# Weight units in another order, small products with a break between their halves, and a bias added by a product, in a mixer-and-experts layer

## The chip, the cores and the metric

The kernel runs on one core of a Trainium2 chip. The metric is the time of one execution on the device in microseconds (us); three runs of the kernel before are given below. The engines go by the names of the profile: PE is TensorE's matmul stream (PEld its loads of weights), DVE is VectorE, ACT is ScalarE, POOL is GpSimd, SP is SyncE, which issues most DMA transfers.

## The reference

The layer works on 256 latent and 256 context tokens of 1024 features, all in fp32. A vector `c` gives six modulation rows (`ada_mod`). Two bidirectional recurrent branches of four heads each (mLSTM and HGRN2) mix the tokens, a gate merges them, and a mixture of 32 experts follows, four per token.

```python
def ada_mod(cvec, w, b):
    return jnp.split(jax.nn.silu(cvec) @ w + b, 6, axis=-1)

# mixer_features: one projection, split into the branches' inputs
    p = h @ w_in + b_in
    mqk, mv, mo, hq, hi, hg, hf, ga, gb, mg = jnp.split(p, SPLIT_POINTS, axis=-1)
    ...
    hi = split_heads(hi, N_HEADS_H).astype(f32)
    z = hf.astype(f32).reshape(B, T, 2, W_H)
    ...
        logf = jnp.logaddexp(jnp.log(lb_d), jnp.log1p(-lb_d) + jax.nn.log_sigmoid(zd))
        kk = (1 - lb_d) * jax.nn.sigmoid(-zd)

# hgrn_scan, per chunk of 32 tokens
        A = jnp.cumsum(fc, axis=2)
        S_new = jnp.exp(AL)[..., None] * S + jnp.einsum('bhsd,bhsv->bhdv', kc * jnp.exp(AL[:, :, None] - A), ic)
        diff = jnp.where(mask[:, :, None], A[:, :, :, None, :] - A[:, :, None, :, :], -jnp.inf)
        s = jnp.einsum('bhtsd,bhsd->bhts', qc[:, :, :, None, :] * jnp.exp(diff), kc)
        o = jnp.einsum('bhts,bhsv->bhtv', s, ic) + jnp.einsum('bhtd,bhdv->bhtv', qc * jnp.exp(A), S)

# layer
        x = x + g1[:, None, :] * rmsnorm(yl, norm_mix_post[l])
        hl = modulate(rmsnorm(x, norm_ffn_pre[l]), sh2, sc2)
        x = x + g2[:, None, :] * rmsnorm(moe_ffn(hl, ...), norm_ffn_post[l])
```

## The kernel before

The mixer takes the first 410 us or so, routing follows, and then the experts' weights stream through until the end. The change lies in the mixer.

**Weight units.** The projection `h @ w_in` is cut into units of 1024 x 256 weights, listed by `unit(...)` and run in that order by the loop of line 1104. A unit's weights are loaded by SyncE, split into a high part (a cast on ScalarE, line 226) and a low part (a difference on VectorE or GpSimd, line 228), and multiplied in two blocks of products (line 237, `mm`). An `hf` block is 24 products of 512 columns; its PSUM bank is emptied by ScalarE (`ev_hf`; for the units of this change line 506, which adds a bias). An `hi` or `mv` block is 48 products of 256 columns, and an `hi` block's bank is emptied by VectorE (`ev_hi`, line 511, a sum into `hi_sb`). A block can begin when one of the rotating banks is empty: two banks named `mm` and, outside the units 7 to 10, the one named `am`.

**Steps of other work.** Behind each block the loop calls `step(n)`, which takes n pieces from the generators in the list `work`, each up to its next `yield`. `hgrn_head(h)` is such a generator. It makes the running sums A (lines 534 and 535) and G on VectorE, differences X (lines 560 and 561), their exponentials on ScalarE (line 562) and products with q and k (lines 582 and 583); the weights' decay Y on ScalarE (lines 567 to 569); then products on TensorE: transposes `trh`, the context's state `so`, the off-diagonal blocks `pts`, and for each of two chunks 44 products of 32 x 32 into `db`, of which VectorE's mask and sum make the diagonal of `pt`; last the output `ho`, emptied into `hmh` (line 639). `to_hgrn` prepares the heads 0 and 1 (on ScalarE: gates and logarithms), `first_heads` puts them into `work`, and `last_heads`, called by `to_last`, does the same for heads 2 and 3 (line 516 is their logarithm).

**Late modulation.** In the units 7 to 10 the generator `ada_rest` makes the last four modulation rows: 16 loads of `w_ada` (line 191) and 16 groups of four products each (line 196) into the bank `am`, eight groups for each half. At the end of a half VectorE adds the bias rows, which lie in `ada_sb`, to the bank (line 855). The first group of the second half needs the bank to be read.

**Engine queues.** Each engine works in the order in which its instructions were written, so a waiting instruction holds back all behind it.

Of the kernel before, what the change touches and what calls it, by code (L numbers as in the profile page):

```python
# [19 lines left out]
KB = 8  # L20
# [44 lines left out]
def layer_kernel(ctx: ExitStack, tc, x, ctxt, w_ada, b_ada, n_mix_post, n_ffn_post, w_in, b_in, w_pa, w_pb, w_out,  # L65
                 w_router, b_router, w_gu, b_gu, w_dn, b_dn, consts, vecs, out, dbg=None):
    nc = tc.nc
# [19 lines left out]
    ident = cp.tile([P, P], F32, name="ident")  # L87
# [103 lines left out]
        nc.sync.dma_start(w, w_ada[k * P:(k + 1) * P, c0:c0 + 2048])  # L191
        return w

    def ada_mm(bank, w, k):
        for j in range(4):
            nc.tensor.matmul(bank[32 * j:32 * j + 32, :], cs[:, k, :], w[:, 512 * j:512 * j + 512],
                             start=(k == 0), stop=(k == KB - 1), skip_group_check=True)

    banks = []

# [243 lines left out]
    work = []  # L444
# [85 lines left out]
    def hgrn_head(h):  # L530
# [82 lines left out]
        pt = hq_.tile([P, 4, P], F32, name="pt", tag="pt", bufs=1)  # L613
        nc.scalar.activation(pt, pts, AF.Identity)
        for ch in range(2):
            db = psm.tile([P, NTERM, 32], F32, name="db", tag="A", bufs=2)
            for tm in range(NTERM):
                for j in range(4):
                    a = ch * P + 32 * j
                    if tm < NTERM - 1:  # L620
                        l_ = r_ = X[:, tm % 2, 2 + tm // 2, a:a + 32]
                    else:
                        l_, r_ = ks[:, a:a + 32], q[:, a:a + 32]
                    nc.tensor.matmul(db[32 * j:32 * j + 32, tm], l_, r_, start=True, stop=True)
            dm = hq_.tile([P, NTERM, 32], F32, name="dm", tag="dm", bufs=1)
            nc.vector.tensor_mul(dm, db, lmask)
            ds_ = hq_.tile([P, 32], F32, name="ds_", tag="ds_", bufs=2)
            nc.vector.tensor_reduce(ds_, dm.rearrange("p n t -> p t n"), AX.X, OP.add)
            for j in range(4):
                sl = slice(32 * j, 32 * j + 32)  # L630
                nc.vector.tensor_copy(pt[sl, 3 * ch, sl], ds_[sl])
# [213 lines left out]
    def ada_rest():  # L845
        for i in range(8):
            nc.gpsimd.dma_start(ada_sb[32 * (i % 4):32 * (i % 4) + 1, i // 4, :],
                                b_ada[2048 + 512 * i:2560 + 512 * i].rearrange("(a b) -> a b", a=1))
        for hf in range(2):
            b = pmm.tile([P, 512], F32, name="am", tag="am", bufs=1)  # L850
            for k in range(KB):
                ada_mm(b, ada_load(2048 + 2048 * hf, k), k)
                if k < KB - 1:
                    yield
            nc.vector.tensor_add(ada_sb[:, hf], ada_sb[:, hf], b)
            yield

    def block_of(a, k):
# [66 lines left out]

    for u in (mq_[1], hf_[0], mk_[0], hf_[1], mk_[1]):
        unit(*u)
    unit(*hi_[0], to_hgrn)
    unit(*hi_[1], None, first_heads)
    unit(*hf_[2])  # L930
    unit(*hf_[3])
    unit(*mv_[0], to_last)
    unit(*mv_[1])

# [169 lines left out]
    for i, u in enumerate(units[1:], 1):  # L1104
# [4 lines left out]
        for j, blk in enumerate(u[1](*cur)):  # L1109
            blk()  # L1110
            for _ in range(rest_at.get((i, j), 0)):
                next(rest)
            if len(convs) > 2 or i > 0 and convs:
                with after(mods[-1:]):
                    convs.pop(0)()
            step(2 if work and len(work) <= 2 or i > 11 else 1)
            for f, *args in load_at.get((i, j), ()):
                if not gu_first:
                    step(100)
                    M["stack"].close()  # L1120
                    vps.close()
                    fps.close()
                    wr1 = pool("wr1", stack=moe)
                    rl = pool("rl", stack=moe)
                    hb0, hb2 = (rl.tile([P, 2, D], BF, name=n) for n in ("hb0", "hb2"))
                f(*args)
# [779 lines left out]
```

## Time and profile before

| | |
|---|---|
| three runs | 1362.54, 1362.87, 1364.57 us; median 1362.87 us |
| profiled execution | 1364.41 us, of which its span is 1362.6 us |
| TensorE busy | 1265.5 us, 93% of the span; mean granted clock 0.981 |
| VectorE, ScalarE, GpSimd busy | 41%, 27%, 10% |
| DMA | 474.12 MB, mean 348 GB/s |

The span goes from the first to the last instruction; 1.8 us of the execution lie outside it. A busy share is an average over stages with different limits, so the stages have to be looked at one by one; the granted clock is the share of full speed that TensorE was given.

### The profile page before, as it was taken

How to read it: one execution, taken by the hardware profiler on the slowest of the kernel's cores; microseconds unless marked ns; L12 is line 12 of the kernel's file. 1: busy time of each engine (PE TensorE's matmuls, PEld its weight loads, DVE VectorE, ACT ScalarE, POOL GpSimd, SP SyncE). 2: the span in 40 equal slices, each digit the busy share in tenths (PEclk: the TensorE clock that was granted, in tenths of full speed). 3: DMA queues.
4: the chain of work that ended last, by engine and by line, in shares of the span. 5: the costliest groups of instructions: out<-in, count | busy, mean ns of one | idle time of the engine just before them, and what ended most of it. 6: DMA issues, size and time to landing. Idle time of an engine off the chain costs nothing. (4 is left out here: it accounts for less than half of the span.)

```text
span 1362.6 us, 20982 instructions
## 1 busy us (share of the span) xinstructions
PE 1265.5 (93%) x8719; PEld 637.9 (47%) x8719; DVE 561.8 (41%) x1211; ACT 361.8 (27%) x712; POOL 129.6 (10%) x140
## 2 busy tenths in 40 slices
PE   4998877999998899999999999999999999999995
PEld 2788665799993333333333333333333333333321
DVE  4699477787666332322222222222222222222224
ACT  3557362446643321111111111211121111211102
POOL 4543335300110000000000000000000000000000
PEclk9999988999999899999999999999999999999997
DMA  9731625745889989999999999999999999999994
GB/s 324 242 102 63 202 78 195 260 135 195 309 304 395 390 367 422 430 424 427 427 427 427 425 392 429 426 426 426 429 424 427 426 428 427 425 428 426 427 420 163
DMA packets 78424, 474.12 MB, mean 348 GB/s; under 512 B 6048, under 2 KB 45480, under 8 KB 50672
## 3 DMA queue, kind: packets, MB, share of 16 engines
q1 hardware_dynamic: 77936, 472.54, 85.7%
q8 instruction: 70, 1.15, 0.3%
q14 instruction: 34, 0.28, 0.1%
q0 software_dynamic: 384, 0.15, 0.0%
HBM read 471.60 MB, written 1.07 MB: 347 GB/s over the span
## 5 line engine op out<-in xcount | busy, mean ns | idle before, releaser
L1609 PE MATMUL pg<-wc,hmh 128*64 128x512 f32 x1048 | 271.8, 598 | 14.9 <-DMA wc<-in_w_gu_dram 14.4
L1609 PE MATMUL pu<-wc,hmh 128*64 128x512 f32 x1048 | 268.9, 592 | 0.0
L1659 PE MATMUL dnl<-wc,hmh 128*64 128x512 f32 x1056 | 236.0, 598 | 9.4 <-ACT hmh L1640 9.1
L1659 PEld LDWEIGHTS dnl<-wc,hmh 128*64 128x64 f32 x1056 | 73.6, 137 | 169.1 <-issue 135.4
L1651 DVE TENSOR_TENSOR ys<-dnl,ys 128x512 fp32r<-128x512 f32 x32 | 22.1, 692 | 307.2 <-ACT ys L1650 307.2
L1609 PEld LDWEIGHTS pu<-wc,hmh 128*64 128x64 f32 x1048 | 74.4, 137 | 150.5 <-issue 150.5
L1620 ACT ACTIVATE scr<-scr 128x512 f32<-128x512 f32 (+1 forms) x34 | 21.0, 619 | 465.8 <-DVE scr L1619 465.8
L1609 PEld LDWEIGHTS pg<-wc,hmh 128*64 128x64 f32 x1048 | 66.9, 136 | 145.5 <-issue 107.4
L1675 DVE SCALAR_TENSOR_TENSOR xr<-sc,wv,xr 128x512 f32<-128x512 f32 x124 | 87.4, 747 | 109.5 <-PE sc L1669 109.5
L1619 DVE TENSOR_SCALAR scr<-pg 128x512 f32<-128x512 f32 (+1 forms) x34 | 22.9, 676 | 219.7 <-PE pg L1609 219.7
L237 PE MATMUL mm<-xh,wp 128*128 128x256 f32 (+1 forms) x576 | 107.7, 332 | 4.2 <-DVE hi_sb L511 3.1
L237 PEld LDWEIGHTS mm<-xh,wp 128*128 128x128 f32 x576 | 88.0, 196 | 14.8 <-issue 4.1
L1385 ACT ACTIVATE hmh<-xp,s2c,a2c 128x64 f32<-128x64 f32 x264 | 81.5, 414 | 38.6 <-PE xp L1581 33.2
L1717 POOL TENSOR_TENSOR scr<-xr,g2n 128x512 f32<-128x512 f32 x2 | 2.5, 1266 | 908.2 <-issue 908.2
L1650 ACT CAST ys<-dnl 128x512 fp32r<-128x512 f32 x32 | 18.7, 585 | 232.3 <-PE dnl L1659 232.3
L1581 PEld LDWEIGHTS <-hb 128*128 128x128 bf16 x960 | 43.7, 98 | 24.3 <-issue 24.3
L228 DVE TENSOR_TENSOR wp<-w,wp 128x2048 fp32r<-128x2048 f32 x21 | 48.0, 2288 | 13.4 <-ACT wp L226 13.4
L237 PE MATMUL mm<-xl,wp 128*128 128x256 f32 (+1 forms) x288 | 53.2, 328 | 0.0
L1669 PE MATMUL sc<-ys,ohT 64*128 64x512 f32 x256 | 48.3, 450 | 4.0 <-DVE xr L1673 3.1
L226 ACT CAST wp<-w 128x2048 fp32r<-128x2048 f32 x25 | 47.5, 1900 | 15.6 <-PE mm L237 8.1
L1581 PE MATMUL xp<-oh,hb 128*128 128x64 bf16 x960 | 47.2, 193 | 0.0
L237 PEld LDWEIGHTS mm<-xl,wp 128*128 128x128 f32 x288 | 44.4, 196 | 4.2
(625 smaller groups left out, 1529.4 us busy)
## 6 DMA issues: line engine op xcount, KB each, us to landing
wc<-in_w_gu_dram SPq DMA_DIRECT2D x119, 2048.0 KB, 25.2
wc<-in_w_dn_dram SPq DMA_DIRECT2D x63, 2048.0 KB, 25.2
w<-in_w_in_dram SPq DMA_DIRECT2D x26, 1024.0 KB, 5.3
w<-in_w_ada_dram SPq DMA_DIRECT2D x16, 1024.0 KB, 4.9
wc<-in_w_gu_dram SPq DMA_DIRECT2D x16, 1024.0 KB, 27.0
aw<-in_w_ada_dram SPq DMA_DIRECT2D x8, 1024.0 KB, 11.7
w<-in_w_pa_dram SPq DMA_DIRECT2D x2, 1024.0 KB, 5.3
w<-in_w_out_dram SPq DMA_DIRECT2D x2, 1024.0 KB, 6.6
```

Source lines behind the costliest of these rows:

```text
L226: nc.scalar.copy(hi, w)
L228: eng.tensor_tensor(lo, w, hi.bitcast(F32), op=OP.subtract)
L237: nc.tensor.matmul(o, ls[k][a], rs[k][b], start=(i + k == 0), stop=(i == 2 and k == n - 1))
L1385: nc.scalar.activation(xg[:, k], xp[k], AF.Identity, scale=a2c[:, k:k + 1], bias=s2c[:, k:k + 1])
L1581: nc.tensor.matmul(xp[:, k], part[:, ch, k * P:(k + 1) * P], oh[:, ch], start=(i == 0), stop=(i == 5))
L1609: nc.tensor.matmul(banks[u][n * g:n * g + n, :], xg[:, k], rows_[:, c0:c0 + W], start=False, stop=(k == KB - 1), skip_group_check=True)
L1619: nc.vector.tensor_scalar(g_, cut(banks[0], i), 7.0, None, op0=OP.min)
L1620: nc.scalar.activation(s_, g_, AF.Sigmoid, scale=1.702)
L1651: nc.vector.tensor_sub(ys[1], b, ys[0].bitcast(F32))
L1659: nc.tensor.matmul(b[64 * hf:64 * hf + 64, :], aT_[:, j, g], dn[g][:, j, hf * 512:hf * 512 + 512], start=(g == 0 and j == 0), stop=(g == 1 ...
L1669: nc.tensor.matmul(s[hf], ohT[ps_, ch * P:(ch + 1) * P], ys[i][ps_], start=(i == 0), stop=(i == 1))
L1675: nc.vector.scalar_tensor_tensor(dst, s[hf], wv[:, ch, col:col + 1], dst, op0=OP.mult, op1=OP.add)
```

## The change

Four edits. The units `hf_[2]` and `hf_[3]` stand ahead of `hi_[0]` and `hi_[1]`, not behind them; `to_hgrn` is called ahead of the first of the moved pair as before of the first of the other, and `first_heads` ahead of `hi_[0]`, where before it was called behind `hi_[1]`. A `yield` stands ahead of each of a head's two runs of 44 small products, so that a head has two pieces more, and in the units 8 to 11 the loop takes three pieces behind a block. In `ada_rest` the bias rows are brought into the bank by a product with the identity ahead of the first group, and ScalarE copies the finished bank, where VectorE added the bias.

```diff
-    def ada_mm(bank, w, k):
+    def ada_mm(bank, w, k, first=True):
         for j in range(4):
             nc.tensor.matmul(bank[32 * j:32 * j + 32, :], cs[:, k, :], w[:, 512 * j:512 * j + 512],
-                             start=(k == 0), stop=(k == KB - 1), skip_group_check=True)
+                             start=(first and k == 0), stop=(k == KB - 1), skip_group_check=True)
...
         for ch in range(2):
+            yield
             db = psm.tile([P, NTERM, 32], F32, name="db", tag="A", bufs=2)
...
             b = pmm.tile([P, 512], F32, name="am", tag="am", bufs=1)
+
+            nc.tensor.matmul(b, ident, ada_sb[:, hf], start=True, stop=False, skip_group_check=True)
             for k in range(KB):
-                ada_mm(b, ada_load(2048 + 2048 * hf, k), k)
+                ada_mm(b, ada_load(2048 + 2048 * hf, k), k, False)
                 if k < KB - 1:
                     yield
-            nc.vector.tensor_add(ada_sb[:, hf], ada_sb[:, hf], b)
+            nc.scalar.copy(ada_sb[:, hf], b)
             yield
...
-    unit(*hi_[0], to_hgrn)
-    unit(*hi_[1], None, first_heads)
-    unit(*hf_[2])
+    unit(*hf_[2], to_hgrn)
     unit(*hf_[3])
+    unit(*hi_[0], first_heads)
+    unit(*hi_[1])
     unit(*mv_[0], to_last)
     unit(*mv_[1])
...
-            step(2 if work and len(work) <= 2 or i > 11 else 1)
+            step(3 if 8 <= i <= 11 else 2 if work and len(work) <= 2 or i > 11 else 1)
```

Line numbers of the changed kernel are one higher from the new `yield` on, and three higher behind `ada_rest`.

**ScalarE, behind head 0's exponentials of X.** Of before: `csg` is a gate of the mLSTM's keys, the cast makes high parts of weights, Y is head 0's decay.

```order
L747 ACT_TABLE_LOAD
L747 ACTIVATE csg<-kT 128x512
L293 ACT_TABLE_LOAD
L226 CAST wp<-w 128x2048
L567 ACTIVATE Y<-A 128x256
L568 ACTIVATE Y<-A 128x128
L569 ACTIVATE Y<-A 128x128
L567 ACTIVATE Y<-A 128x256
L568 ACTIVATE Y<-A 128x128
L569 ACTIVATE Y<-A 128x128
L226 CAST wp<-w 128x2048
L506 ACTIVATE lf_660<-mm,cols 128x512
```

And of the change, at the same place:

```order
L748 ACT_TABLE_LOAD
L748 ACTIVATE csg<-kT 128x512
L293 ACT_TABLE_LOAD
L506 ACTIVATE lf_660<-mm,cols 128x512
L226 CAST wp<-w 128x2048
L567 ACTIVATE Y<-A 128x256
L568 ACTIVATE Y<-A 128x128
L569 ACTIVATE Y<-A 128x128
L567 ACTIVATE Y<-A 128x256
L568 ACTIVATE Y<-A 128x128
L569 ACTIVATE Y<-A 128x128
L506 ACTIVATE lf_660<-mm,cols 128x512
```

The emptyings of `hf` banks (line 506) have moved ahead: the second of them stands ahead of the cast, the third directly behind Y. The first product of the unit `hi_[0]` waits for the third.

**TensorE, small products of heads 0, 1 and 2.** Before, at head 0, with the first product of its output behind:

```order
L624 MATMUL db<-xr 32x32 x40
L624 MATMUL db<-hqT,ks 32x32 x4
L624 MATMUL db<-xr 32x32 x40
L624 MATMUL db<-hqT,ks 32x32 x4
L635 MATMUL ho__1604<-hi_sb,pt 128x128
```

And of the change, at head 0:

```order
L625 MATMUL db<-xr 32x32 x40
L625 MATMUL db<-hqT,ks 32x32 x4
L625 MATMUL db<-xr 32x32 x40
L625 MATMUL db<-hqT,ks 32x32 x4
L237 MATMUL mm<-wp,xh 128x256 x8
```

A block of an `hi` unit follows where the output followed; the 88 products of head 0 stand together as before. Of the change, at the beginning of head 1's:

```order
L625 MATMUL db<-xr 32x32 x14
L596 MATMUL so<-hi_sb,kt 128x128 x4
L600 MATMUL pts<-Y 128x128
L625 MATMUL db<-xr 32x32 x19
L601 MATMUL pts<-Y 128x128
L605 MATMUL pts<-xr 64x64
```

And of the change, at head 2's, with groups of the late modulation (`am`) and blocks of an `mv` unit:

```order
L625 MATMUL db<-xr 32x32 x17
L196 MATMUL am<-w,cs 32x512 x4
L625 MATMUL db<-xr 32x32 x23
L625 MATMUL db<-hqT,ks 32x32 x4
L237 MATMUL mm<-wp,xh 128x256 x8
L237 MATMUL mm<-wp,xl 128x256 x4
L196 MATMUL am<-w,cs 32x512 x4
L237 MATMUL mm<-wp,xl 128x256 x4
L237 MATMUL mm<-wp,xh 128x256 x16
L237 MATMUL mm<-wp,xl 128x256 x8
L237 MATMUL mm<-wp,xh 128x256 x8
L625 MATMUL db<-xr 32x32 x33
```

The products of head 1 and head 2 stand in pieces now. In the kernel before, those of head 1 stand together, as those of head 0 do.

**VectorE, at head 2's differences X.** Of before, around the first read of an `mv` block's bank into `v_sb`:

```order
L560 TENSOR_TENSOR xr<-A 128x2x64
L561 TENSOR_TENSOR xr<-A 128x2x64
L560 TENSOR_TENSOR xr<-A 128x4x32
L561 TENSOR_TENSOR xr<-A 128x4x32
L560 TENSOR_TENSOR xr<-A 128x8x16
L757 TENSOR_TENSOR v_sb<-mm,bvi 128x2x128 x2
L561 TENSOR_TENSOR xr<-A 128x8x16
L560 TENSOR_TENSOR xr<-A 128x16x8
```

And of the change, from head 2's first running sum on:

```order
L534 SCALAR_TENSOR_TENSOR A<-scm_667,lf_660 128x256
L541 SCALAR_TENSOR_TENSOR G<-cons_669,lf_660 128x255
L560 TENSOR_TENSOR xr<-A 128x2x64
L535 SCALAR_TENSOR_TENSOR A<-scm_668,lf_660 128x256
L542 SCALAR_TENSOR_TENSOR G<-cons_669,lf_660 128x255
L561 TENSOR_TENSOR xr<-A 128x2x64
L560 TENSOR_TENSOR xr<-A 128x4x32
L758 TENSOR_TENSOR v_sb<-mm,bvi 128x2x128 x2
L561 TENSOR_TENSOR xr<-A 128x4x32
```

The read into `v_sb` stood behind 19 of the 28 differences, and now stands behind three.

## Rows read from the trace of the kernel before

**Rows 1.** Windows: length; busy PE, PEld, DVE, ACT, POOL (instructions); clock, DMA share, GB/s

```profile
110.00:260.00 150.00, 124.62 (x1544) 99.78 (x1542) 110.66 (x296) 66.82 (x94) 67.14 (x80) 0.93 0.47 160
300.00:410.00 110.00, 109.67 (x906) 108.52 (x905) 77.45 (x167) 62.26 (x95) 10.12 (x5) 1.00 0.72 257
490.00:1345.00 855.00, 828.84 (x5138) 296.49 (x5134) 217.54 (x376) 127.45 (x335) 0.00 (x0) 1.00 1.00 422
```

**Rows 2.** Waits of TensorE from 110 to 260 us: total, times, longest

```profile
PE db L624 <- issue: 7.4, 3, 4.6
PE mm L237 <- DVE hi_sb L511: 5.4, 2, 3.1
```

**Rows 3.** Timeline of TensorE at 219 us: start, duration, then the idle before

```profile
219.11 1.94 PE L196 MATMUL am<-w,cs 128*32 128x512 f32 x8 [6.30 <-DVE ada_sb L855]
```

**Rows 4.** Timeline of TensorE, weight units from 103 to 143 us

```profile
103.32 3.79 PE L237 MATMUL mm<-xh,wp 128*128 128x512 f32 x16
108.76 1.98 PE L237 MATMUL mm<-xh,wp 128*128 128x512 f32 x8
...
127.41 1.12 PE L237 MATMUL mm<-wp,xl 128*128 128x256 f32 x8
128.37 1.12 PE L237 MATMUL mm<-wp,xh 128*128 128x256 f32 x8
...
142.43 3.60 PE L237 MATMUL mm<-xh,wp 128*128 128x512 f32 x8 [3.10 <-DVE hi_sb L511]
```

**Rows 5.** Timeline of ScalarE from 134 us, and the emptying of a bank

```profile
134.46 1.28 ACT L293 ACT_TABLE_LOAD   x1
...
139.36 1.88 ACT L226 CAST wp<-w 128x2048 fp32r<-128x2048 f32 x1
...
149.74 0.69 ACT L506 ACTIVATE lf<-mm,cols 128x512 f32<-128x512 f32 x1 [8.50 <-PE mm L237]
```

**Rows 6.** Timeline of TensorE, an fp32 product of 256 columns

```profile
267.83 1.02 PE L775 MATMUL sA<-qT,kT 128*128 128x256 f32 x4
268.50 1.30 PE L237 MATMUL mm<-xh,wp 128*128 128x256 f32 x8
```

**Rows 7.** Timeline of TensorE, the small products of heads 0 and 1

```profile
168.74 0.75 PE L624 MATMUL db<-xr 128*32 128x32 f32 x60
...
174.08 0.48 PE L624 MATMUL db<-xr 128*32 128x32 f32 x18 [4.59 <-issue]
...
194.85 0.47 PE L624 MATMUL db<-xr 128*32 128x32 f32 x34 [2.46 <-issue]
...
198.22 0.39 PE L638 MATMUL ho__1880<-hi_sb,pt 128*128 128x128 f32 x2
```

**Rows 8.** Window from 175 to 180 us, columns as in rows 1

```profile
175.00:180.00 5.00, 5.00 (x21) 4.57 (x21) 4.93 (x22) 1.28 (x5) 1.15 (x2) 0.51 0.02 5
```

**Rows 9.** DMA from 171 to 172 us: queue, packets, MB, share

```profile
q8 instruction: 1, 0.02, 5.7%
```

**Rows 10.** Timelines of GpSimd and VectorE from 202 to 219 us

```profile
202.21 6.64 POOL L228 TENSOR_TENSOR wp<-w,wp 128x2048 fp32r<-128x2048 f32 x1 [5.91 <-ACT wp L226]
...
203.87 0.29 DVE L561 TENSOR_TENSOR xr<-A 128x128 f32<-128x128 f32 x1
204.94 4.07 DVE L561 TENSOR_TENSOR xr<-A 128x128 f32<-128x128 f32 x1
...
218.39 0.67 DVE L855 TENSOR_TENSOR ada_sb<-ada_sb,am 128x512 f32<-128x512 f32 x1
```

**Rows 11.** Timelines of ScalarE and VectorE around 197 us

```profile
196.56 0.28 ACT L639 ACTIVATE hmh<-ho__1874 128x128 f32<-128x128 f32 x1 [1.16 <-PE ho__1874 L638]
196.73 1.51 ACT L516 ACTIVATE lf<-lf,lb,olb 128x512 f32<-128x512 f32 x2
...
198.10 0.69 DVE L534 TENSOR_TENSOR_SCAN A<-scm,lf 128x256 f32<-128x256 f32 x1
```

**Rows 12.** Window from 220 to 260 us, columns as in rows 1

```profile
220.00:260.00 40.00, 35.87 (x615) 26.28 (x607) 27.90 (x83) 12.23 (x19) 17.73 (x29) 0.95 0.68 230
```

## The prediction

> **What bounds the kernel now.** I read the windows by stage first. From 490 to 1345 us the transfers of the experts' weights fill the DMA engines (share 1.00) beside a TensorE that is busy 97% of the time; from 300 to 410 us TensorE is busy 109.67 of 110 us; but from 110 to 260 us it is busy only 124.62 of 150, at a mean clock of 0.93 [rows 1]. These 25.4 us of idle time, and what is lost at half clock behind the longest of them, are all that this change can win from, since everything it touches stands there. A shift at 260 us passes through the full stretch behind it, and the weight streams wait for slots that TensorE's products free, so I pass it on to the end one to one.
>
> The waits of TensorE in that stretch come next. Three kinds make up 19 of the 25 us: 7.4 us in which `db` products wait for nothing the profile shows ("issue") and 5.4 us in two waits of `mm` products for VectorE's `hi_sb` sums [rows 2], and one wait of 6.30 us of the late modulation's product `am` for VectorE's sum on line 855 [rows 3]. Each is touched by one part of the change, so I go part by part, always asking where TensorE stands with the same work done.
>
> **The weight units.** Before, the first unit behind the two `hi` units starts at 142.43 us, after an idle of 3.10 us for a bank that an `hi_sb` sum has to empty, and its first eight products take 3.60 us [rows 4] where eight of them otherwise take 1.81 (24 in 5.44 us, from 103.32 to 108.76): 1.8 us go at half clock. With `hf` units in this place the banks are emptied by ScalarE, so the wait does not vanish, it moves to ScalarE's queue. The order of ScalarE's instructions shows the third emptying (line 506), for which the first product of the moved `hi` unit waits, behind a table load, the second emptying, a cast and six Y exponentials. By the rows of before [rows 5] the table load ends at 135.74 (134.46 and 1.28); the second emptying adds 0.69; cast and Y, which fill the time up to the next cast at 139.36, take 3.62; the third emptying adds 0.69: 140.74. So TensorE resumes at 140.8 instead of 142.43, **+1.6 us** (plus is earlier), after an idle of some 8 us, because the `hf` products ahead are done at 132.3 (108.76, one third of a block, and four blocks of 5.44); the half clock behind it I leave as it was.
>
> The `hi` blocks now stand where full-rate `hf` blocks stood. Eight products of 256 columns take 0.96 us (127.41 to 128.37), a block of 48 takes 5.76, against 5.44 for an `hf` block of 24 [rows 4]. Four blocks change places in front of the late heads: **-1.3 us**. They were 1.3 us shorter on the way to 140.8, but that is swallowed in the wait there.
>
> **The bias by a product.** One product of the bias rows with the identity (128 x 512, fp32) is added ahead of each half. The nearest row is the fp32 product `sA` of 256 columns: two calls (four records) take 0.67 us from their start to the next group's, 1.02 us to their modelled end [rows 6]; 512 columns are the same columns. I take 0.7, bounds 0.5 and 1.0, since both starts lie on a full TensorE: **-0.7 us** for the first.
>
> **Head 0's burst.** In the order, its 88 `db` products still stand one behind the other: the new yield stands there, but no block lands in it, only behind all 88. So the 4.59 us of "issue" before 174.08 [rows 7] stay, I think, and only what follows gains: before, small `ho` products and a block ran at a granted clock of 0.51, the lower of TensorE's two levels (1.2 GHz), for five microseconds [rows 8], 2.5 us lost; now a block of `hi` products follows at once. I give that **+0.5 us**. What the stall is can be seen beside it: 60 of the small products take 0.75 us together [rows 7], nothing is waited for, and in the microsecond from 171 to 172 the DMA view has a packet of the instruction queue, of 0.02 MB [rows 9]. So I read it as instructions that run out, and whose packet comes late.
> The Trainium skill ("Runtime: NRT & Kernel Launch", section "Instruction fetch mechanics") says that instructions come in blocks of 16 KiB, 256 of them, and that crossing into the next is "mostly hidden". The trace agrees on the packet's size and disagrees on the rest, with 4.59 us. By the rule alone splitting a burst could bring nothing; by the row it could bring up to 4.59.
>
> **Head 1's burst** is really split: the first 33 of its 88 products stand ahead, among `so` and `pts`. Before, 2.46 us are lost to "issue" ahead of 194.85 [rows 7]. Its first 33 products now wait for VectorE's X products, and the emptying of an `hi` block stands among those on VectorE; I cost that wait at as much as the fetch saves, **0**, with bounds of 2 us either way. The last `ho` of head 1, at 198.22 before [rows 7], then comes at 198.1: 1.6 - 1.3 - 0.7 + 0.5 = +0.1.
>
> **The late modulation's second half** restarts TensorE at 219.11 after 6.30 us [rows 3]. It waits for VectorE's sum at 218.39, which stands behind a scan and behind head 2's X products, and these are late because a subtraction at 204.94 takes 4.07 us instead of 0.29 while GpSimd's 6.64 us split of weights runs [rows 10]. Two things pull against each other.
> Earlier: the new copy on ScalarE stands directly behind head 2's second exponential, without the scan (0.6 us less). And VectorE's first read of PSUM, `v_sb`, behind which the 4.07 us fall, moves ahead of nearly all subtractions, where GpSimd's split has perhaps not begun: 3.8 us less.
> Later: before, line 516 began at 196.73, right behind the first `hmh` (0.28 us at 196.56) [rows 11]. Now it stands behind the second, a sigmoid of its own size (0.75) and a table load (1.28): the last `ho` ends at 198.1 + 0.4, and with 0.28 + 0.75 + 1.28 that makes 200.8; the first of line 516's pair adds 0.75, so head 2's first scan, which ran at 198.10 [rows 11], runs at 201.6: 3.5 us more.
> Together 219.1 - 0.6 - 3.8 + 3.5 = 218.2; bounds 215.3 (only the 3.8 tell) and 222.0 (only the 3.5, less the 0.6). I take 218.2, **+0.9**; all that was lost or gained ahead is in it. But nine products of 256 columns (1.1 us) that before lay ahead of the wait now lie behind it, and so does the second identity product: **-1.1 and -0.7**.
> The Trainium skill ("SBUF — State Buffer", section "SBUF: two separate sides") calls the port that VectorE and GpSimd share an exclusive lock, held for the whole instruction by whoever starts first. The 4.07 and 6.64 us agree with it, and by it everything hangs on who is first at the moved read.
>
> **Behind it.** From 220 to 260 us TensorE idles 4.13 us [rows 12], in small waits of heads 2 and 3. Head 2's products now stand in pieces of 17, 27, 33 and 11 with blocks or `am` groups between, and three steps per block bring head 3 forward: I keep 1.6 of the 4.13, **+2.5**. The mLSTM's gates, which follow, have a filler less to wait beside, by my guess **-0.3**.
>
> **Sum:** +0.9 - 1.1 - 0.7 + 2.5 - 0.3 = +1.3 us of the profiled execution's 1364.41, which makes 1363.1. That execution is 1.5 us above the median of the three runs, 1362.87, and I take the gain from the median: **1361.6 us**. That is half of 0.2% (2.7 us), below which a measurement of this kernel can't tell it from no change.
>
> **Rivals.** (A) The sum, between 1359 and 1364.
> (B) Head 0's packet comes sooner. The loads of the `am` weights, behind which it may stand, shift with the `am` groups, and a fetch like head 1's would cost 2.46 instead of 4.59. For it: head 1. Against: SyncE's order is unchanged and the burst starts within a microsecond of where it did. All behind it, head 2 too, comes 2.1 us earlier: 1359.5.
> (C) The lock misses and line 516 isn't late, so the second half restarts at 215.3: 2.9 us more, 1358.7; with B 1356.6. For it: `v_sb` stands near the front now. Against: GpSimd's split waits for a cast that stands behind line 516 and can meet the X products instead.
> (D) Slower: ScalarE's queue. Line 516 is late by 3.5 us, GpSimd's lock falls on the subtractions all the same, and the restart is 222.0: 3.8 us off, and half of the 2.5 behind it gone with head 2's lateness: 1361.6 + 5.0 = 1366.6. It decides from a restart at 219.5, where the sum is zero.
> (E) Nothing arrives: one wait gives its time to the next, or the weight streams swallow it, as their DMA share of 1.00 allows: 1362.9.
>
> **Chances.** A 0.44, B 0.15, C 0.20, D 0.14, E 0.07. B and C are faster, with 0.05 of A: 0.40. Of A 0.37 is within 0.2%, 0.02 slower; with E and 0.02 of D that makes 0.46 the same and 0.14 slower. The range goes from B and C together, with a microsecond of unknown bounds, 1355.5, nearly to D, 1366.0.
>
> **What would show it.** In the profile of the changed kernel: the product behind the third line 506 starts near 140.8, after an idle of about 8 us that ScalarE ends; no wait for line 511 is left there; a stall of about 4 us called "issue" remains in head 0 and almost none in heads 2 and 3; an identity product takes 0.5 to 1.0 us; the second half restarts near 218, released by ScalarE's copy. The prediction is wrong if TensorE's idle time between 110 and 260 us shrinks by over 5 us, if head 0's stall is gone, or if the restart lies outside 215 to 222.

## The result, and the profile after

The change makes the kernel slower: **1373.77 us** median (five runs, 1372.13 to 1374.04) against 1363.16 of before in the same session (five runs, 1362.54 to 1366.69), a ratio of 1.0064 with a 95% interval of 1.0051 to 1.0077. The ratio is estimated from the single runs and is not the quotient of the medians (1.0078): by its interval the change costs 7.0 to 10.5 us, and the medians' 10.6 is at the upper end. The forecast was 1361.6, its range ended at 1366.0. The profiled execution took 1372.13 us (span 1370.3) against 1364.41: 7.7 us more.

The windows after, in the columns of [rows 1]:

```profile
110.00:260.00 150.00, 122.42 (x1500) 96.57 (x1498) 106.54 (x276) 64.84 (x92) 70.14 (x80) 0.90 0.45 156
300.00:410.00 110.00, 109.80 (x901) 108.39 (x900) 77.25 (x171) 60.84 (x88) 10.65 (x5) 1.00 0.72 253
490.00:1345.00 855.00, 831.22 (x5152) 297.27 (x5148) 219.05 (x377) 127.89 (x335) 0.00 (x0) 1.00 1.00 424
```

These windows don't hold the same work before and after, since the two executions are not level where the changed part begins. The last products that both have in common start at 108.76 before [rows 4]; in the change TensorE is there 3.4 us sooner. ScalarE and VectorE are 1.8 us sooner, as `csg` shows, first of the change, then of before:

```profile
105.37 1.98 PE L237 MATMUL mm<-xh,wp 128*128 128x512 f32 x8
```

```profile
124.14 0.63 ACT L748 ACTIVATE csg<-kT 128x512 f32<-128x512 f32 x1 [5.56 <-DVE kT L664]
```

```profile
125.90 0.63 ACT L747 ACTIVATE csg<-kT 128x512 f32<-128x512 f32 x1 [5.56 <-DVE kT L663]
```

No edit of the change concerns the products up to there. The profiles of the other kernels lie between 3.4 us ahead of before and 0.1 behind it at this place, and not by their edits: e5 and e12, with the same products, lie 1.5 us ahead and 0.1 behind. Windows of the same work go from there to the router's first product, before and after:

```profile
108.76:411.99 303.23, 274.71 (x2729) 246.26 (x2727) 220.12 (x536) 148.76 (x222) 77.26 (x85) 0.96 0.58 199
```

```profile
105.37:418.36 312.99, 279.69 (x2733) 249.05 (x2731) 221.10 (x541) 151.81 (x226) 80.79 (x85) 0.94 0.56 193
```

The change takes 9.8 us more for the same work: TensorE idles 4.8 us more (33.3 against 28.5) and is busy 5.0 us longer, at a clock of 0.94 instead of 0.96. Two losses, then: waiting, and a lower clock. TensorE's waits after (total, times, longest), from 100 to 300 us, against [rows 2, 3], which are the same from 100 to 300 us:

```profile
PE mm L237 <- ACT lf L506: 8.0, 2, 7.7
PE db L625 <- issue: 7.4, 2, 4.0
PE trh L588 <- POOL G L545: 6.1, 1, 6.1
PE db L625 <- DVE xr L583: 3.3, 1, 3.3
PE tg L735 <- DVE gi__2652 L719: 2.2, 1, 2.2
```

The wait for `hi_sb` is gone, and ScalarE's is there in its place, as forecast. But "issue" (idle time in which TensorE waits for nothing that the profile shows) is 7.4 us as before, and the 6.30 us of `am` for VectorE's sum have become 6.1 of the transposes `trh` for GpSimd's G. The timeline of TensorE shows where:

```profile
138.89 2.08 PE L237 MATMUL mm<-wp,xh 128*128 128x256 f32 x8 [7.73 <-ACT lf L506]
...
146.27 1.02 PE L853 MATMUL am<-ada_sb,ident 128*128 128x512 f32 x2
147.22 1.07 PE L196 MATMUL am<-w,cs 128*32 128x512 f32 x8
...
171.79 0.26 PE L625 MATMUL db<-hqT,ks 128*32 128x32 f32 x5 [4.04 <-issue]
...
187.41 0.53 PE L625 MATMUL db<-xr 128*32 128x32 f32 x20 [3.27 <-DVE xr L583]
...
198.75 0.49 PE L639 MATMUL ho__1881<-hi_sb,pt 128*128 128x128 f32 x2
...
218.16 1.43 PE L588 MATMUL trh<-ident,G 128*128 128x128 f32 x4 [6.12 <-POOL G L545]
220.55 0.80 PE L600 MATMUL pts<-Y 128*128 128x128 f32 x2 [0.96 <-POOL Y L572]
221.14 1.91 PE L853 MATMUL am<-ada_sb,ident 128*128 128x512 f32 x2
222.98 1.71 PE L196 MATMUL am<-w,cs 128*32 128x512 f32 x8
...
261.77 0.32 PE L625 MATMUL db<-xr 128*32 128x32 f32 x9 [3.33 <-issue]
...
418.36 1.08 PE L1345 MATMUL pg<-bgu,ident 128*64 128x512 f32 x4 [0.79 <-DVE gmoh L1236]
...
1355.95 1.46 PE L1715 MATMUL sc<-wc,ohT 64*128 64x512 f32 x8 [0.68 <-ACT wc L1707]
```

And of before, the places that answer to the last three:

```profile
255.88 0.22 PE L624 MATMUL db<-xr 128*32 128x32 f32 x2 [0.33 <-issue]
...
411.99 1.08 PE L1342 MATMUL pg<-bgu,ident 128*64 128x512 f32 x4 [0.79 <-DVE gmoh L1233]
...
1348.25 1.46 PE L1712 MATMUL sc<-wc,ohT 64*128 64x512 f32 x8 [0.68 <-ACT wc L1704]
```

The last two are the marks that I use below: `pg`, the router's first product, and `sc`, the last product of all. The change is 6.4 us late at `pg` and 7.7 late at `sc`, against a profile that it led by 1.8 to 3.4 us at the start. The loss is made in the mixer; little comes behind it. In the profiled execution of before, head 3's burst (its runs of small products `db`) waited 0.33 us; in the change it waits 3.33 us.

Why `trh` waits at 218 is read from GpSimd, ScalarE and VectorE, one timeline each, against [rows 10, 11]:

```profile
206.20 11.18 POOL L228 TENSOR_TENSOR wp<-w,wp 128x2048 fp32r<-128x2048 f32 x1 [8.44 <-ACT wp L226]
217.34 1.50 POOL L545 TENSOR_TENSOR G<-G,kks 128x256 f32<-128x256 f32 x2
```

```profile
201.39 2.93 ACT L516 ACTIVATE lf<-lf,lb,olb 128x512 f32<-128x512 f32 x4
204.23 1.89 ACT L226 CAST wp<-w 128x2048 fp32r<-128x2048 f32 x1
...
212.63 0.56 ACT L858 COPY ada_sb<-am 128x512 f32<-128x512 f32 x1
```

```profile
202.23 0.69 DVE L534 TENSOR_TENSOR_SCAN A<-scm,lf 128x256 f32<-128x256 f32 x1 [3.02 <-ACT lf L516]
...
205.17 0.75 DVE L758 TENSOR_TENSOR v_sb<-mm,bvi 128x256 f32<-128x256 f32 x2
...
212.91 0.77 DVE L758 TENSOR_TENSOR v_sb<-mm,bvi 128x256 f32<-128x256 f32 x2
213.58 3.95 DVE L582 TENSOR_TENSOR xr<-xr,hqT 128x128 f32<-128x128 f32 x1
```

Line 516 is late, as forecast (201.39, estimated 200.8), and four of it now stand ahead of the cast whose result GpSimd splits. So the split starts at 206.20, one microsecond behind the start of VectorE's first read of PSUM (205.17) and ahead of 35 operations with two SBUF inputs that VectorE runs back to back, from 205.84 to 212.9. It ends 3.8 us after VectorE's next read of PSUM. Before, too, the split ended 3.9 us after such a read [rows 10]. So I take it that of its 11.18 us it did not get on for some seven. ScalarE's copy of the bank was done at 213.2, six microseconds sooner than VectorE's sum [rows 10], and helped nothing, since identity product and `am` stand on TensorE's queue behind `trh` and `pts`.

### The profile page after: what moved, and what is told of

Its sections match the earlier page's. It is cut to its first block, busy times and chain, and to the rows that moved or that the text cites. A ratio compares the mean times of both kernels' runs of the same rounds, so it can differ in the third digit from the quotient of the medians.

```text
span 1370.3 us, 20994 instructions
## 1 busy us (share of the span) xinstructions
PE 1269.4 (93%) x8723; PEld 638.4 (47%) x8723; DVE 559.0 (41%) x1209; ACT 363.3 (27%) x714; POOL 134.8 (10%) x140
## 5 line engine op out<-in xcount | busy, mean ns | idle before, releaser
L237 PE MATMUL mm<-xh,wp 128*128 128x256 f32 (+1 forms) x576 | 103.1, 325 | 2.2 <-DVE xh L331 1.0
L237 PE MATMUL mm<-wp,xh 128*128 128x256 f32 x256 | 38.7, 298 | 7.7 <-ACT lf L506 7.7
```

Source lines behind the costliest of these rows:

```text
L237: nc.tensor.matmul(o, ls[k][a], rs[k][b], start=(i + k == 0), stop=(i == 2 and k == n - 1))
```

## The experiments

Lags are against the profile of before at the same product, `pg` and `sc`; times are medians, each ratio is to before in the same session (1363.88, 1364.18, 1363.93 and 1363.84 us). "Start" is the lag at the last products that all have in common. The clock is that of TensorE from 110 to 300 us in the profiled execution, 0.94 before and 0.90 in the change; "issue" is 7.4 us in both. Lags, clock and "issue" are of one execution, which can lie some 3 us off the median (e10 1366.29, e7 1377.40). The change and e11 run the same products up to `pg`, and so do e5 and e12; their lags there differ by 1.9 and 1.2 us.

| kernel | us | ratio, 95% interval | lag start, `pg`, `sc` | clock | "issue", 100 to 300 us |
|---|---|---|---|---|---|
| e1 halves | 1368.93 | 1.0038, 1.0024-1.0052 | -1.0, +3.0, +5.2 | 0.92 | 4.8 |
| e2 bias | 1371.53 | 1.0062, 1.0041-1.0083 | -2.0, +3.5, +7.8 | 0.93 | 9.6 |
| e3 order | 1372.06 | 1.0075, 1.0050-1.0101 | -3.4, +4.7, +6.7 | 0.92 | 10.0 |
| e8 order, bias | 1370.89 | 1.0048, 1.0031-1.0064 | +0.1, +6.2, +6.2 | 0.91 | 9.7 |
| e4 change, split moved | 1377.92 | 1.0101, 1.0077-1.0125 | -0.6, +10.7, +15.4 | 0.89 | 7.8 |
| e7 change, late half first | 1374.52 | 1.0076, 1.0056-1.0096 | -2.2, +10.5, +13.1 | 0.89 | 7.5 |
| e11 change, gaps filled | 1370.56 | 1.0048, 1.0034-1.0063 | -3.1, +8.3, +8.0 | 0.91 | 7.4 |
| e6 before, shifted | 1365.66 | 1.0012, 1.0001-1.0023 | (see text) | (see text) | 2.7 |
| e9 order, shifted | 1363.14 | 1.0001, 0.9992-1.0010 | -3.2, -2.5, -2.7 | 0.95 | 1.1 |
| e10 halves, shifted | 1369.73 | 1.0047, 1.0032-1.0062 | -1.7, +0.6, +2.1 | 0.92 | 0 |
| e15 bias, shifted | 1364.58 | 1.0008, 0.9996-1.0020 | -0.4, -3.7, -1.0 | 0.95 | 0.6 |
| e13 order, halves, shifted | 1366.86 | 1.0022, 1.0009-1.0036 | -1.9, +1.0, +3.3 | 0.91 | 0 |
| e14 order, bias, shifted | 1366.63 | 1.0019, 1.0008-1.0031 | -2.7, -1.2, +0.3 | 0.94 | 2.4 |
| e5 change, shifted | 1369.35 | 1.0041, 1.0026-1.0056 | -1.5, +2.6, +7.5 | 0.92 | 0.3 |
| e12 change, shifted, filled | 1369.67 | 1.0036, 1.0024-1.0047 | +0.1, +3.8, +6.2 | 0.91 | 0.2 |

**The parts alone.** e1 has the `yield` and the three steps of the diff, e2 the identity product and the copy, e3 the new order of the units; e8 is the change without the halves. The rivals were GpSimd's split with what stands behind it on TensorE's queue (theory 1), ScalarE's queue (theory 2) and the identity products (theory 3).

> The kernel before with the halves of the small products and the three pieces per block alone. Theory 1 (the pieces brought forward put head 2's transposes and first pts products ahead of the late modulation's second half on TensorE, and these wait for GpSimd's starved split of weights): 4 to 9 us slower than before, 1367 to 1372, with one long wait of TensorE for GpSimd's G near 215 us. Theory 2 (the order of the weight units costs it: the wait for ScalarE's emptying and line 516 that comes late): within 3 us of before. Theory 3 (the products with the identity cost it): within 3 us of before.

> The kernel before with the bias by a product alone. Its order has the second identity product ahead of head 2's transposes. Theory 1: the bank is read by ScalarE some 3 to 6 us before VectorE's sum read it (219.1), the second half starts near 213 to 217, and the whole is 1 to 4 us faster than before, 1359 to 1362. Theory 2: within 3 us of before. Theory 3: 2 to 6 us slower, 1365 to 1369.

> The kernel before with the order of the weight units alone. Theory 1: within 3 us of before (a wait of 7 to 8 us for ScalarE near 131 us takes the place of the two for hi_sb, 5.4 us). Theory 2: 6 to 10 us slower, 1369 to 1373. Theory 3: within 3 us of before.

Each part alone costs 5 to 8 us, while the whole change costs 10.6: the parts don't add up, and none of the three theories explains all of them. The order alone lies where theory 2 has it, but not for its reason: head 1's last `ho` comes 3.1 us sooner than before, which is the 3.4 of the start, so up to there the order cost nothing, in spite of the 8 us of waiting for ScalarE. The loss comes behind it, and most of it at head 3's burst: at the 15th `am` group e3 is still 3.2 us ahead of before, and at head 3's first `ho` it is 2.4 us late. A wait called "issue" of 2.98 us stands there, 0.33 before. The bias alone, which theory 1 expected to be faster than before, has such a wait of 3.41 us there.

So I looked at where these waits lie. I counted all of TensorE's records in the trace, weight loads, products and its sequencer's waits. In every unshifted kernel, the waits of about 2 us and more between 100 and 300 us lie at three counts, 1985, 2497 and 4033 (4034 in some), which differ by multiples of 256, whatever part of a burst stands there. Not every kernel has all three: the second is gone in each kernel with the halves and there in before, e2, e3 and e8; the third is there in each kernel with the order or the identity products, and not in before and e1. Head 3's is the clearest. Before, a packet of the instruction queue comes between 253 and 254 us, where SyncE issues 1 MB loads (line 210) at 253.46. The DMA view of before from 253 to 254 us, and SyncE's row:

```profile
q8 instruction: 1, 0.02, 5.5%
```

```profile
253.46 2.48 SPq L210 DMA_DIRECT2D w<-in_w_in_dram  x2
```

In the change, SyncE issues the same two loads at 254.96, and the next packet is found between 259 and 260 us only, among theirs:

```profile
254.96 3.35 SPq L210 DMA_DIRECT2D w<-in_w_in_dram  x2
```

```profile
q1 hardware_dynamic: 286, 0.28, 103.0%
q8 instruction: 1, 0.02, 6.7%
```

By the count of the records, TensorE reaches a new block of 256 at 253.41 before and at 256.34 in the change. Before, that is 0.05 us ahead of the load, and the packet starts 0.06 us later; in the change the load was ahead, the packet starts 2.9 us later, and the burst ran through its 256 in about 2. The other unshifted kernels repeat it at this block: in e1 the crossing comes 0.04 us ahead of the load and the packet 0.08 us behind the crossing; in e2, e3, e8, e4, e7 and e11 the load is 0.5 to 2.1 us ahead of the crossing, and the packet comes 2.5 to 3.3 us behind it. This became theory 4: a wait arises where a block is crossed within a burst, so that the next ends before a packet that a load delays. It is a matter of where the counts fall, and of no part of the change by itself. That a packet is asked for at the crossing is inferred: where products had just been waiting, a packet can start ahead of the crossing (in the change at 188.46, with the crossing at 190.31).

The Trainium skill ("DMA: Bandwidth & Descriptors", section "Issuing engines are not separate DMA queues") says that DMAs started by ScalarE, SyncE or GpSimd run on the same 16 engines and interleave. It says nothing there of instruction packets; these rows show one among the loads' packets.

**Counts shifted.** If theory 4 holds, tiny products at the program's start, whose results nothing reads, must take these waits away. Each makes four records, and n is 32 to 48, another one in each kernel:

```diff
+        for _ in range(n):
+            nc.tensor.matmul(tcol[0:32, 0, 0:32], ident[0:32, 0:32], ident[0:32, 0:32], start=True, stop=True)
         for i, n in ((1, 112), (0, 116)):
             nc.tensor.transpose(tcol[:, i, 0:n], rows[0:n, i * P:(i + 1) * P], ident[0:n, 0:n])
```

> The whole change, with 48 products of 32 x 32 of the identity ahead of the first transposes, at 4 to 14 us, where TensorE is idle (their result is overwritten). They move all later instructions of TensorE by some 192 places, so that its blocks of 256 begin elsewhere in the heads. Theory 4 (the issue waits in heads 0 and 3 fall exactly where a block of 256 TensorE instructions ends whose successor was asked for behind a 1 MB load): the issue waits fall from 7.4 us to under 3, the one of 3.3 us in head 3 is gone with the half clock behind it, and the kernel is 4 to 9 us faster than the change as it is, 1364 to 1369. Theory 1 (GpSimd's starved split decides) and theory 2 (ScalarE's queue decides): within 2 us of the change as it is, 1371 to 1375.

> The kernel before, with 38 such products, which move its blocks by some 152 places. Theory 4: the issue waits of heads 0 and 1, 4.59 and 2.46 us, shrink to 2 to 4 together, and what stays depends on whether a packet is asked for ahead of a load; 0 to 5 us faster than before, 1358 to 1363. Theories 1 and 2: within 2 us of before.

> The whole change but for the halves and the third piece per block. In its order the second identity product stands ahead of head 2's transposes by itself. Theory 1: 4 to 9 us faster than the change as it is, 1364 to 1369. Theory 4: issue waits in heads 0, 1 and 3 of 8 to 10 us together, as with the order alone and the bias alone: 1370 to 1376. Theory 2: 1371 to 1375.

> The new order of the units alone, with 36 tiny products (144 records) ahead of the first transposes, so that the places at which TensorE's instructions run into their next block of 256 lie elsewhere. With the order alone the mixer stood 3.1 us ahead at the end of head 1 and lost that and 4 us more to three waits called issue (10.0 us). Theory 4 (blocks that end in a burst of products) expects issue waits under 4 us, the first router product (411.99 before, 416.7 with the order alone) 1 to 4 us ahead of before, and a time of 1360 to 1367. Theory 2 (ScalarE's queue, 8 us at its third emptying) expects the order to cost the same wherever the blocks end: 1369 to 1373. If the granted clock behind the router falls below 0.9 between 415 and 435 us, up to 4 us of a gain are lost there (theory 5).

The order alone becomes 8.9 us faster by 36 tiny products, and is then no slower than before; theory 2 falls, since ScalarE's wait is still there. The waits of e9:

```profile
PE mm L237 <- ACT lf L508: 8.1, 2, 7.8
PE am L196 <- DMA w<-in_w_ada_dram: 6.3, 2, 5.8
PE ho__2670 L640 <- DVE pt L633: 2.0, 1, 2.0
...
PE am L196 <- issue: 0.8, 1, 0.8
```

The bias alone becomes 7.0 us faster (below). For these two theory 4 is shown. In the whole change the waits go as well (0.3 us of "issue" left of 7.4), and it becomes 4.4 us faster by the medians (e5 against 1373.77); but 1369.35 lies just above theory 4's range, and the intervals of the two ratios overlap. The profiles bear the gain out: from the start to `pg` the change and e11 take 313.0 and 314.6 us, e5 and e12 with the same products 307.4 and 306.9. Where waits are left in a shifted kernel, they too lie at a multiple of 256 records from the first three, to within one: 2.7 us in e6 at count 3522, 1.9 us in e14 at 2754.

Theory 4 missed two. The halves alone gain nothing by the medians (1368.93 and 1369.73), though 4.8 us of "issue" went, and before itself nothing either (e6). The profiled execution of e6, 1374.78 us at a mean granted clock of 0.939, stands apart from its other ten (1363.07 to 1367.28), so I read no lags from it. Its idle time from the start to `pg` is 28.3 us, as before's is 28.5, though "issue" fell from 7.4 to 2.7: other waits took its place (that for `hi_sb` is 6.9 us instead of 5.4). Whether that is so in the other ten stays open.

One control is missing: 64 tiny products, a whole block of 256 records, which should leave the waits in place. What speaks against another effect of the tiny products is that they run from 3.5 to 7.5 us in e9, ahead of a wait for weights that lasts until 12.9, and that the shifted kernels are as early at the start as the others.

e8, unshifted, still has its 9.7 us of "issue", as theory 4 expected, and is not as much faster for the lack of halves as theory 1 had it.

**Which part costs what is left?**

> The halves alone, with 40 tiny products (160 records) ahead. Theory 4 expects no issue wait over 1 us, the first router product at or ahead of before's 411.99 (with the halves alone 415.0), and 1362 to 1368. Theory 1 (GpSimd's starved split and what stands behind it on TensorE's queue, 4.2 us in the halves alone) expects that wait to stay and 1366 to 1371 whatever the blocks do.

> The order of the units and the halves, without the identity products, shifted by 48 tiny products (192 records) so that no block ends in a burst. The order alone so shifted is 1363.14, the whole change so shifted 1369.35, the halves alone so shifted 1369.73. If the halves are what costs (theory 1: the late half of the modulation stands on TensorE's queue behind head 2's trh, which waits 5 to 6 us for GpSimd's split), this is 1367 to 1371 with that wait of 5 to 6 us in it. If the identity products cost (theory 3), it is 1362 to 1365.

> The order of the units and the identity products, without the halves, shifted by 44 tiny products (176 records). If the halves cost (theory 1), this is like the order alone so shifted: 1362 to 1366, with no wait over 3 us of trh for GpSimd's split. If the identity products and their copies cost (theory 3), 1367 to 1371. Issue waits may remain, of up to 5 us together, since no shift frees all bursts here (theory 4).

> The identity products alone, shifted by 32 tiny products (128 records). Unshifted they were 1371.53 with 9.6 us of issue waits. Theory 4 expects 1363 to 1367 with under 3 us of them; theory 3 (the products and copies cost by themselves, 3.7 us of waiting for ScalarE's copy among it) 1368 to 1372.

Between kernels without these waits the parts can be compared: order 1363.14, with the halves 1366.86, with the bias 1366.63 (2.4 us of "issue" remain in it), with both 1369.35. The halves add 3.7, the identity products at most 3.5, and together they add 6.2, each to within some 2 us by the intervals of the ratios; each kernel was run at one shift only. The bias alone is 1364.58, within the noise of before: theory 3 falls for it, and e14 lies between the two theories' numbers. e10 lies where theory 1 has it, and above theory 4's numbers. Theory 1 missed e13 by 0.1 us, and its wait is there. Of e13, waits, and the window from its start to its `pg`:

```profile
PE mm L237 <- ACT lf L508: 8.0, 2, 7.7
PE trh L590 <- POOL G L547: 5.2, 1, 5.2
PE pts L602 <- POOL Y L574: 2.9, 2, 2.0
```

```profile
106.84:412.98 306.14, 277.34 (x2730) 246.72 (x2728) 219.90 (x543) 150.66 (x224) 79.82 (x85) 0.94 0.57 198
```

And the window of the same work in e9:

```profile
105.59:409.50 303.91, 273.93 (x2729) 244.79 (x2727) 224.70 (x543) 150.94 (x224) 73.59 (x85) 0.97 0.58 199
```

GpSimd's split at head 2 takes 10.4 to 11.2 us in the eight kernels with halves that leave it on GpSimd, and 5.5 to 8.1 in the eight without halves. Yet TensorE's idle time is no longer with the halves than without them (28.8 and 30.0 us in these windows): `trh`'s wait for the split stands where `am`'s for its weights stood. What differs is the busy time, 3.4 us longer for the same products, at a clock of 0.94 against 0.97. The halves alone show the same against before (e1: 28.1 us idle against 28.5, busy 4.5 us longer). So I don't put the 3.7 us down to the wait itself but to the time that TensorE runs at the lower of its two levels (1.2 GHz); that is an argument from these rows, and no run held the clock fixed.

**Two tries at theory 1's wait.** e4 keeps the split from GpSimd; e7 puts the late half's first products ahead of head 2's `trh` and `pts`, with one more of its groups behind an earlier block:

```diff
-    on_pool = (5, 7, 11)
+    on_pool = (5, 7)
```

```diff
+                with after(late_first if h == 2 else []):
                     nc.tensor.transpose(tr[:, d, ch], G[:, d, ch * P:(ch + 1) * P], ident)
...
-    rest_at = {..., (9, 0): 2, (9, 1): 3, ...}
+    rest_at = {..., (9, 0): 3, (9, 1): 2, ...}
```

> The whole change, and the split of weights that takes GpSimd 11.18 us near 206 us made on VectorE (as most splits are, 2.3 us each). Theory 1: GpSimd's G is there 4 to 8 us sooner, the wait of 6.1 us for it at 218 us is gone or under 2 us, and the kernel is 3 to 7 us faster than with the change as it is, 1366 to 1370. Theories 2 and 3: within 2 us of the change as it is, 1371 to 1375.

> The whole change, with the second identity product and the first group of the late modulation's second half ahead of head 2's transposes and pts products on TensorE, so that they need not wait for GpSimd's G. Theory 1: the identity product starts near 213 us, right behind ScalarE's copy, and not at 221; 2 to 5 us faster than the change as it is, 1369 to 1372. Theory 4: head 2 ends at the same time or up to 3 us sooner, but head 3's block of instructions ends where it did, so the total depends on whether its packet meets the load: 1366 to 1375. Theory 2: no difference, 1371 to 1375.

Both are slower. In e4 `trh` still waits 4.7 us, since now GpSimd's own `G` stands in VectorE's stretch; in e7 the identity product starts at 216.57, but the first `am` group behind it waits 7.9 us for its weights. Both lie outside what theory 1 expected, and neither tells what the change would take without the wait.

**The clock behind the router.** From `pg` to `sc` the change loses another 1.3 us, e5 even 4.8. Behind `pg` the router's products stand singly, with waits of 0.97, 0.87 and 0.69 us, in before as in the change. The product that follows these waits, before and in the change:

```profile
422.67 1.07 PE L1342 MATMUL pu<-bgu,ident 128*64 128x512 f32 x2
```

```profile
429.03 1.92 PE L1345 MATMUL pu<-bgu,ident 128*64 128x512 f32 x2
```

From 425 to 435 us the granted clock is 0.83 in the change and 0.56 in e5; before it is 1.00 throughout this stretch. That this costs the time behind `pg` is theory 5 of the expectations. e11 and e12 put transposes of the identity, which nobody reads, into these waits:

```diff
+    spare = psm.tile([P, 4, P], F32, name="spare", tag="A", bufs=2)
+    fill(spare, 5)
...
     first_tokens(fb_, oh0f, 0)
+    fill(spare, 4)
...
     token_slots(1)
+    fill(spare, 4)
```

> The change with thirteen transposes of the identity into a spare bank, put between the router's products, where TensorE waits 0.97, 0.87 and 0.69 us. Theory 5 (the clock falls to its lower level in the sparse stretch of the router, and half a rate behind it loses time that before did not lose): granted clock 1.00 from 425 to 440 us (0.75 to 0.91 in the change), the lag behind before of 6.4 us at the first router product stays 6.4 at 508 us instead of 8.9, and the time is 2 to 3 us under the change's, 1370 to 1372. Without theory 5 the fillers change nothing or cost up to 1 us: 1373 to 1375.

> The change with both: 48 tiny products ahead (no block ends in a burst) and the thirteen transposes in the router's gaps. Theories 4 and 5 together expect 4 to 5 us less than the shifted change's 1369.35, so 1363.5 to 1366.5, no different from before; the lag at the first router product of 2.6 us stays 2 to 3.5 at 508 us (7.4 without the transposes). Without theory 5: 1368 to 1371.

In both the clock stays 1.00, and e11 loses nothing behind `pg` (+8.3, +8.0). It is 3.2 us faster than the change by the medians, as theory 5 had it; but medians of two sessions are compared here, and the intervals of the ratios overlap, so this is not shown. e12 missed: it is no faster than e5. In its profile 2.4 us are lost behind `pg`, most of it at the very end, where the last expert's products wait for "issue" and an instruction packet starts 2.7 us ahead of the wait's end:

```profile
1351.76 1.97 PE L1672 MATMUL dnl<-wc,hmh 128*64 128x512 f32 x4 [2.08 <-issue]
```

A shift that frees one place can spoil another. None of these kernels is shown to be faster than before.

## Why the forecast was wrong

**Weight units: right.** TensorE resumes at 138.89 instead of 140.8, released by the third line 506. ScalarE's table load ended at 134.0, where my sum had 135.7. But these 1.8 us are those by which ScalarE was ahead from the start, so the better number is luck, and the sum along ScalarE's queue was right. The first `am` group starts at 147.22 against 149.64 before, 2.4 us sooner.

**Identity products: the first within the bounds, the second not.** The first takes 0.95 us (146.27 to 147.22), forecast 0.7 with bounds 0.5 and 1.0. The second takes 1.84 us at a granted clock of 0.50; that it would run at the lower level was not in the sum.

**Head 0: right.** 4.04 us of "issue" remain. **Head 1: within the bounds.** The fetch wait of 2.46 is gone, and a 3.27 us wait for an X product is there; forecast was 0, with 2 either way. The last `ho` comes at 198.75, forecast 198.1; without the lead at the start that is 2.4 to 4.0 us later than forecast. I can't put that down to one term: e4 and e11, with the same products up to there, have their last `ho` 0.6 us ahead of before's and 1.7 behind it.

**Late modulation: wrong, the first step that failed.** The forecast had the second half restart at 218.2, "released by ScalarE's copy". The copy was ready at 213.2, but the identity product came at 221.14 and the first `am` group at 222.98, 3.9 us later than before in spite of the lead at the start, where the forecast had a gain of 0.9 less 0.7 for the identity product. TensorE did resume at 218.16, the forecast number, but that is luck: with `trh`, released by GpSimd. I had not asked what stands between the copy and `am` on TensorE's own queue. Before, head 2's `trh` stood ahead of the restart too, and did not wait:

```profile
211.14 0.60 PE L588 MATMUL trh<-ident,G 128*128 128x128 f32 x4
```

In the kernels without the halves, `trh` has no such wait for G; in those with them it waits 4.2 to 6.1 us, but for e7, which moves it. With the bias alone (e2) the copy does release the restart, 2.3 us sooner than before:

```profile
216.77 2.08 PE L852 MATMUL am<-ada_sb,ident 128*128 128x512 f32 x2 [3.68 <-ACT ada_sb L857]
```

I had also taken the read into `v_sb` near the front as a gap in which GpSimd gets on, worth 3.8 us; the split missed it by one microsecond and waited for the next. Rival C's doubt, that the split "can meet the X products instead", is what happened, and rival D's restart of 222.0 is the nearest number.
The Trainium skill ("SBUF — State Buffer", section "SBUF: two separate sides") has the lock go to whichever of VectorE and GpSimd starts first, for the whole instruction. That agrees with VectorE's 3.95 us behind the split. The rows show the other side as well: the split waiting some seven microseconds through VectorE's operations of 0.3 each.

**Behind it, +2.5: the wrong sign, the second step that failed.** I had kept 1.6 of the 4.13 us of idle time there; from 222.98 to head 3's last `ho` at 267.7 TensorE idles 6.7 us. Head 3's `db` burst waits 3.33 us of them in "issue", where before it had waited 0.33. Halves and three steps per block were to shorten the waits of heads 2 and 3. Head 1's wait is gone with the halves, but head 3's came with the order or the identity products (it is there in e2, e3 and e8 without halves, and not in e1): 7.4 us of "issue" in all both times. I had read the stall as a late packet, which the counts bear out, but as a property of the burst. It is one of the burst's place among the blocks of 256 and the loads.

**A shift at 260 us passes on one to one: not quite.** 6.4 us at `pg` became 7.7 at `sc`. And the medians differ by 10.6, where the profiled executions differ by 7.7: the change's had the lead at the start and was the fastest of its five. Executions of one kernel scatter with their mean clock: e10's six go from 1366.29 us at 0.979 to 1372.72 at 0.973. The change's five lie at 0.976 to 0.977, and the profiled one of before at 0.981.

**The sum.** Of the 10.6 us by the medians, 4.4 go when the counts are shifted (e5). The halves and the identity products add 3.7 and at most 3.5 to the order alone, which, shifted, takes no longer than before. I can't say for sure why before's own fetch waits cost it nothing that a shift would give back, nor how much of the halves' 3.7 is the clock.

## What to carry to other kernels

Where TensorE runs bursts of products of some 10 ns each, find the "issue" waits in the trace, count the instructions ahead of them, and see which loads stand ahead of the instruction packet. Some dummy products at the start can tell whether a change of several microseconds is the edit's or the counts'. Test an edit at two such shifts before judging it, and before with it. Compare two profiles over the same work, from a place ahead of the edit, and not over the same stretch of time. And a result that comes sooner is worth nothing until one has read what stands between it and its reader on the reader's queue.

## What the runs showed of the hardware

- Instruction packets came late behind loads. At the block ahead of head 3's burst the packet started 0.06 and 0.08 us behind the crossing in the two unshifted kernels where 1 MB loads were issued just after it (before, e1), and 2.5 to 3.3 us behind it in the seven where a load had been issued 0.5 to 2.1 us ahead.
- TensorE's waits in "issue" during bursts lay at multiples of 256 records from each other, and 36 tiny products at the start moved one kernel by 8.9 us (e3 and e9).
- GpSimd's split of 128x2048 at head 2 took between 5.5 and 11.2 us, by where it met VectorE's operations with two SBUF inputs. In e4, two 128x256 products on GpSimd, 1.50 us otherwise, took 12.2 us there.
- Behind waits of 0.97, 0.87 and 0.69 us among the router's single products, TensorE's granted clock fell to its lower level (1.2 GHz) in some kernels (the mean from 425 to 435 us is 0.56 in e5) and stayed at 1.00 in others (before, e8, e9), with the same products and the same waits.
